# Seven block products in place of eight for the U and Z groups 0 to 3 of a hybrid decoder layer's input projection, made for two token tiles at a time

## The chip, the cores and the metric

The kernel runs on one core of one Trainium2 chip. The metric is the device time of one execution in microseconds (us), the median of several runs. The profile, taken by the hardware profiler, is of one such execution. The engines are called as in the profile: PE is TensorE (matrix products; PEld are its weight loads), DVE is VectorE, ACT is ScalarE, POOL is GpSimd, and SP is SyncE, whose queue issues nearly all DMA transfers here. L12 is line 12 of the kernel's file. Lines of the changed kernel are named as such, since its file is longer.

## What is computed

One decoder layer on 2048 tokens of width 1024, in f32. The part that the change touches is the input projection and the gMLP group; the rest is named because its work runs in the same stretches.

```
h = rms_norm(x, pre_norm_g)                       # (2048, 1024)
proj = h @ w_in                                   # 1024 -> 3072 columns
a_u, a_v, sq, sk, sv, mq, z = split(proj, [512, 512, 256, 128, 128, 256, 1024])
y_a = chunked_spatial_gating(gelu(a_u), gelu(a_v), ...)      # (2048, 512)
y_b = sliding_window_attention(sq, sk, sv, ...)              # (2048, 256)
y_c = memory_cross_attention(mq, mem_k, mem_v)               # (2048, 256)
y = concat(y_a, y_b, y_c) * silu(z)               # (2048, 1024)
x = x + rms_norm(y @ w_out, post_norm_g)

def chunked_spatial_gating(u, v, ...):            # chunks of 128 tokens, 4 groups of 128 channels
    vhat = layer norm of v over each group, with gain and bias
    sv = einsum('gts,bnsgc->bntgc', tril(w_s), vhat) + b_s
    return u * sv
```

So for the channel groups g = 0 to 3 of 128 channels each, the output part is y = gelu(U_g) * sv_g * silu(Z_g), where U_g and Z_g are products of h with 128 columns of `w_in`. These eight products (four U, four Z) for every token are what the change computes in another way. The other four Z groups (4 to 7) belong to the two attentions.

## The kernel before

**Tiles and stages.** The 2048 tokens are worked in four tiles of 512 (`TS`, `NT`). In phase 1 each tile t goes through the same list of products: V (96 matmuls of 128x512, L752), then the groups sv, k, q0, q1, mq0, mq1, z4, z5 (tile 0 has four small projections of the memory tokens here, L427), then U_g, a small product sg (four 128x128 matmuls, the spatial gating) and Z_g for g = 0 and 1, z6, z7, and the same for g = 2 and 3. A group (`group`, L321) is one bank of 128 channels by 512 tokens, made by 24 matmuls: eight chunks of the 1024 input channels, and for each three passes, because every f32 operand is split into a rounded part ("hi") and the rest ("lo") and hi·hi, hi·lo and lo·hi are summed. `split` makes the two parts: ACT casts hi (L91), DVE or POOL subtracts for lo (L92). Between every six matmuls of a group there is a slot (`slot`, L855): a table (`A_SLOTS`) puts pieces of the attention units of this tile there, four window units and eight memory units, whose softmax is done by DVE and ACT between two pieces.

**The normalised input.** h of a tile is kept, split, in one of two buffers `hTs`. For the next tile it is made in eight chunks of 128 channels (`make_h`, L306: a product on DVE with the row of 1/rms values, called `bcs`, then a split). The 1/rms values are computed by token, stored to DRAM (`rstd_d`, L257) and loaded back, broadcast to all partitions, as `bcs` (L261). `NEXT_STATS`, `LOADS` and `MAKES` are tables of slots for these steps.

**The weights.** Each group's weights come as one unit of 128x1024. In tile 0 (V of tile 1) a unit is loaded raw (`wraw`), split into a ring of four buffers of 1 MB (`whl`) and stored split to DRAM (`split_d`, L181); in later tiles it is loaded split (L146). When a unit is begun, `weight_unit` (L166) asks for the one three units on.

**The elementwise end of a group.** U_g goes through a gelu (`gelu2`) and Z_g through a silu (`silu2`), both shared by ACT and DVE; DVE multiplies gate, U and Z (L896, L899), and the result is stored to DRAM (`yd`).

**Phase 2**, the output projection (L1123), reads `yd` and already works two tiles at a time with seven products of blocks in place of eight, 672 matmuls in all. Its weight operands, differences of blocks of `w_out`, are made in tiles 1 and 2 (`weight_operands`, L617), and the sums of y for its first pair in tile 3 (`first_sums`).

**What sets the order.** The order on PE and on the SP queue is the order in which the program is written. In phase 1 DVE, ACT and POOL are ordered by a scheduler ahead of the run; in phase 2 all are ordered as written. Each engine works its own list strictly in that order, and an instruction that waits holds up those behind it.

## Time and profile before

| what | value |
|---|---|
| median of three runs | 763.64 us (763.6, 763.64, 764.14) |
| span of the profiled execution | 762.2 us |
| PE busy | 753.2 us, 99% of the span, 3700 matmuls |
| DVE busy | 562.8 us, 74%, 1056 instructions |
| ACT busy | 396.9 us, 52% |
| POOL busy | 110.7 us, 15%, 122 instructions |
| tile 0 / 1 / 2 / 3 / phase 2 / tail | to 167.7 / 144.9 / 145.0 / 144.8 / 152.4 / 7.4 us |
| DMA | 194 MB, mean 254 GB/s |

The profiled execution's own time is its span, 762.2 us, and the 1.4 us to the median lie around the span. The page gives the busy time of each engine and the chain of work that ended last, followed back from the last instruction; the table of waits says which engine stood still for what; the windows give busy time for chosen stretches; a group row of the page or of the lines view gives how often one instruction was run, its busy time and its mean duration. Matmuls are pipelined, so that the mean duration in such a row is not the time from one matmul to the next.

### The profile page before, as it was taken

The numbers are of one execution on the slowest core, as the hardware profiler recorded it, in microseconds if no ns is written. First come the engines' busy times: TensorE is split into PE (matmuls) and PEld (weight loads), VectorE is DVE, ScalarE is ACT, GpSimd is POOL, SyncE is SP. The second block draws the span as 40 slices with busy tenths as digits, with TensorE's granted clock in tenths as the row PEclk, the third lists the DMA queues.
The fourth block names the chain that finished last, engine by engine and source line by source line (L and its number), as shares of the span: only waits on it lengthen the run. The fifth ranks groups of instructions, "written<-read, shape, count | busy, mean of one in ns | idle before, by whom it ended". The sixth has DMA issues, their size and how long they took to land.

```text
span 762.2 us, 10453 instructions
## 1 busy us (share of the span) xinstructions
PE 753.2 (99%) x3700; PEld 634.1 (83%) x3700; DVE 562.8 (74%) x1056; ACT 396.9 (52%) x865; POOL 110.7 (15%) x122
## 2 busy tenths in 40 slices
PE   9999999999999999999999999999999999999996
PEld 7878988888888888888888888888888888888884
DVE  6396889996658878754888788748976325885787
ACT  7687775654735654455465544644443233443341
POOL 0556221000203200011032000201300000020002
PEclk9999999999999999999999999999999999999999
DMA  9847387987477897927678968664574699937734
GB/s 331 306 159 278 131 288 244 346 306 279 145 263 275 296 322 287 314 79 276 229 269 301 345 233 343 200 244 164 156 246 149 223 397 398 362 104 283 277 137 193
DMA packets 54068, 193.95 MB, mean 254 GB/s; under 512 B 5468, under 2 KB 6017, under 8 KB 44801
## 3 DMA queue, kind: packets, MB, share of 16 engines
q1 hardware_dynamic: 53488, 192.70, 71.0%
q8 instruction: 29, 0.48, 0.3%
q10 hardware_dynamic: 528, 0.59, 0.2%
q14 instruction: 23, 0.18, 0.1%
HBM read 140.84 MB, written 52.44 MB: 254 GB/s over the span
## 4 chain that ended last, share of the span: by engine, by line
PE 99%; DVE 0%; issue 0%; DVEq 0%; POOL 0%; ACT 0%; ACTq 0%; POOLq 0%
PE g_z L321 23%; PE v L752 12%; PE g_u L321 12%; PE g_q L321 6%; PE g_mq L321 6%; PE Y_S L1123 6%; PE Y L1123 6%; PE X_S L1123 6%; PE g_k L321 3%; PE X L1123 3%; PE g_sv L321 3%; PE l_b L497 2%; PE l_c L550 2%; PE o_b L532 2%; PE o_c L579 2%; PE sg L891 2%
## 5 line engine op out<-in xcount | busy, mean ns | idle before, releaser
L321 PE MATMUL g_z<-hT,whl 128*128 128x512 f32 x768 | 190.8, 396 | 0.0
L321 PEld LDWEIGHTS g_z<-hT,whl 128*128 128x128 f32 x768 | 139.6, 188 | 26.5
L321 PE MATMUL g_u<-hT,whl 128*128 128x512 f32 x384 | 96.5, 395 | 0.0
L752 PE MATMUL v<-whl,hT 128*128 128x512 f32 x384 | 89.4, 393 | 0.0
L752 PEld LDWEIGHTS v<-whl,hT 128*128 128x128 f32 x384 | 72.8, 190 | 15.8 <-ACT whl L91 0.6
L321 PEld LDWEIGHTS g_u<-hT,whl 128*128 128x128 f32 x384 | 69.9, 188 | 13.4
L91 ACT CAST whl<-wraw 128x1024 fp32r<-128x1024 f32 (+1 forms) x43 | 44.2, 1027 | 33.1 <-DMA wraw<-in_wst 15.3
L191 POOL TENSOR_TENSOR rsr_v<-rsa_v,mhalf 128x4 f32<-128x4 f32 x16 | 16.7, 1056 | 224.8 <-DVE mv L777 130.8
L321 PE MATMUL g_q<-hT,whl 128*128 128x512 f32 x192 | 45.9, 394 | 0.0
L92 DVE TENSOR_TENSOR whl<-wraw,whl 128x1024 fp32r<-128x1024 f32 (+1 forms) x30 | 35.5, 1183 | 12.7 <-ACT whl L91 12.5
L321 PE MATMUL g_mq<-hT,whl 128*128 128x512 f32 x192 | 44.7, 389 | 0.0
L1123 PE MATMUL Y_S<-hT,yop_S 128*128 128x512 f32 x192 | 44.2, 389 | 0.0
L1123 PE MATMUL Y<-hT,yop 128*128 128x512 f32 x192 | 43.8, 389 | 0.0
L522 POOL TENSOR_SCALAR_AFFINE_SELECT pT_b<-pT_b 128x512 fp32r<-128x512 f32 x30 | 21.3, 710 | 147.4 <-ACT pT_b L91 147.4
L1123 PEld LDWEIGHTS Y<-hT,yop 128*128 128x128 f32 x192 | 36.0, 188 | 7.5
L1123 PEld LDWEIGHTS Y_S<-hT,yop_S 128*128 128x128 f32 x192 | 36.0, 188 | 7.5
L321 PEld LDWEIGHTS g_q<-hT,whl 128*128 128x128 f32 x192 | 35.8, 188 | 7.8 <-ACT KK L91 0.2
L560 ACT ACTIVATE L_c<-l_c,nm_c 128x256 f32<-128x256 f32 x48 | 22.4, 471 | 37.8 <-DVE nm_c L555 37.8
L321 PEld LDWEIGHTS g_mq<-hT,whl 128*128 128x128 f32 x192 | 35.8, 188 | 7.3
L1028 POOL TENSOR_TENSOR r<-a,mhalf 128x1 f32<-128x1 f32 x16 | 13.5, 845 | 191.7 <-DVE a L1026 185.7
L92 POOL TENSOR_TENSOR whl<-wraw,whl 128x1024 fp32r<-128x1024 f32 x13 | 31.6, 2439 | 31.7 <-ACT whl L91 31.3
L992 DVE TENSOR_TENSOR yop<-y,yop 128x1024 fp32r<-128x1024 f32 x12 | 14.6, 1219 | 24.0 <-ACT yop L983 24.0
(211 smaller groups left out, 1427.1 us busy)
## 6 DMA issues: line engine op xcount, KB each, us to landing
whl<-split_d SPq DMA_DIRECT2D x50, 1024.0 KB, 6.3
wraw<-in_wst SPq DMA_DIRECT2D x41, 512.0 KB, 5.7
split_d<-whl SPq DMA_DIRECT2D x18, 1024.0 KB, 7.1
hT<-wo_B SPq DMA_DIRECT2D x10, 1024.0 KB, 8.7
wo_T<-hT SPq DMA_DIRECT2D x8, 1024.0 KB, 9.0
y<-yd SPq DMA_DIRECT2D x7, 1024.0 KB, 10.9
xj<-in_xT SPq DMA_DIRECT2D x12, 512.0 KB, 8.5
xs<-in_x SPq DMA_DIRECT2D x24, 256.0 KB, 5.6
```

Of the source, the lines that this page charges most:

```text
L91: a = nc.scalar.copy(hi, src)
L92: b = (lo_engine or nc.vector).tensor_tensor(lo, src, f32(hi), ALU.subtract)
L191: nc.gpsimd.tensor_tensor(r, a, mhalf[:, :c], ALU.pow)
L321: nc.tensor.matmul(ps, w[:, wi, k * P : (k + 1) * P], hT[:, hi, k, :], start=(n == 0), stop=(n == 3 * KC - 1))
L497: nc.tensor.matmul(lg[:, e, :], S[kv][:, e, c * P : (c + 1) * P], KK[:, kv, s, c * P : c * P + 256], start=(s == 0), stop=(s == 1))
L522: nc.gpsimd.affine_select(prev[:, s], f32(own[:, s]), [[0, 4], [-1, P]], ALU.is_gt, 0.0, base=0, channel_multiplier=1)
L532: nc.tensor.matmul(o[:, kv, :], SV[:, c + w, kv].rearrange("p a b -> p (a b)"), pT, start=(n == 0), stop=(n == len(terms) - 1))
L550: nc.tensor.matmul(lg[:, e, :], S[:, h % 2, q0 : q0 + P], MK[:, h, s, :], start=(s == 0), stop=(s == 1))
L560: last = nc.scalar.activation(p[:, e, :], lg[:, e, :], AF.Exp, bias=nm[:, e : e + 1], scale=scale, accum_out=den[:, e : e + 1])
L579: nc.tensor.matmul(o, MV[:, j, h].rearrange("p a b -> p (a b)"), pT[:, s, j].rearrange("p a b -> p (a b)"), start=(n == 0), stop=(n == 3))
L752: nc.tensor.matmul(vps[i], hT[:, hi, 2 * j + kk, i * P : (i + 1) * P], w[:, wi, kk * 512 : (kk + 1) * 512], start=(j == 0 and (hi, wi, kk) ...
L1123: nc.tensor.matmul(banks[m], a(s, k)[:, m * P : (m + 1) * P], w(v, k), start=first and n == 0, stop=n == 11, skip_group_check=not first)
```

## The change

U_g and Z_g for g = 0 to 3 are no longer made tile by tile. After tile 1, and again after tile 3, one function (`set_a`) makes them for both tiles of the pair. The weights are seen as a 2x2 matrix of blocks (U or Z, first or second half of the 1024 input channels), and h likewise (first or second half of the channels, first or second tile). The product of the two is made by seven block products, in the form of Strassen's scheme that Winograd gave, each with 4 groups x 12 matmuls of 128x512: 336 matmuls for a pair, where 2 tiles x 8 groups x 24 = 384 stood. Four of the seven are accumulated one after the other in the same four banks, with copies taken between; the last three are interleaved by group and end in the gelu, silu and products.

What else this brings with it:

- Sums and differences of the weight blocks, four 128x512 operations on POOL per group (`weight_sums`), made once, stored to DRAM (`tu_d`, `tz_d`) and read back in both sets. The 14 weight units of a set are loaded raw and split each time.
- Sums and differences of blocks of h (`h_sums`), 32 operations of 128x512 per pair, shared by POOL and DVE; three of the four sums are stored to DRAM and read back (12 transfers of 256 KB each way for a pair), and all four are split again.
- h of both tiles of a pair has to be held, so the two buffers become four half-buffers and a spare, and h of tile 0, overwritten by the memory's, is made a second time in tile 1.
- The normalised V (`vhat`) is stored to DRAM, by ACT's queue, and read back for the sg products, which now stand inside the set.
- The weight ring has three buffers, and in tile 0 the spare as a fourth. `weight_unit` refills the buffer of the unit that has just been used.
- For t > 0 the product of the softmax with 1/denominator goes from DVE to POOL (`normalise`). Gate·U·Z goes from DVE to POOL (`times`). The output projection's weight differences, now all in tile 2, and the sums of y in phase 2 go from DVE to POOL as well.
- The order of the seven products in phase 2 is another, and two of its first y operands are made in tile 3.
- The tables of slots are new. The first tile has eight groups fewer after its memory projections, so that h of tile 1 is made at its slots 32 to 42, where V of tile 1 begins at slot 36; before, the row of 1/rms values was loaded at slot 52, h made from slot 60, and V began at slot 68.

```diff
-NEXT_STATS = (16, 4)
-LOADS = ((46, 46, 48, 48, 53, 55, 65, 65), (34, 34, 36, 36, 43, 45, 57, 57))
-MAKES = ((60, 62, 64, 66, -28, -28, -24, -24), (50, 52, 55, 57, -28, -28, -24, -24))
+N_SLOTS = (36, 84, 28, 84)
+NEXT_STATS = (-8, 10, -23)
+MAKES = ((32, 33, 35, 36, 38, 39, 41, 42), (66, 68, 70, 72, 76, 79, 85, 88), (20, 22, 24, 26, 29, 31, 33, 35))
...
+LAST_SEQ = (("T1", 0), ("B21", 0), ("T1", 1), ("B22", 0), ("B21", 1), ("T1", 2),
+            ("B22", 1), ("B21", 2), ("T1", 3), ("B22", 2), ("B21", 3), ("B22", 3))
+FIRST_OPS = ("B11", "T2", "T3", "T4")
+SEQ_A = tuple((op, g) for op in FIRST_OPS for g in range(4)) + LAST_SEQ
...
-        while halved[0] < min(i + 4, len(order)):
+        if i - 1 in in_use:
+            place = in_use.pop(i - 1)
+            if place is not spare_ring or order[i][1] == 0:
+                free.append(place)
+        while halved[0] < len(order) and free:
...
+    def normalise(t, last, p, den, shape):
+        r = nc.vector.reciprocal(den, den)
+        scaled = (nc.gpsimd if t else nc.vector).tensor_tensor(p, p, den[:, :, None].broadcast_to(shape), ALU.mult)
+        queue_aside(last, r if t else scaled)
...
+    def weight_sums(g):
...
+        def difference(into, i, a, ia, b, ib):
+            c = [slice(512 * x, 512 * x + 512) for x in (i, ia, ib)]
+            nc.gpsimd.tensor_tensor(r[into][:, c[0]], r[a][:, c[1]], r[b][:, c[2]], ALU.subtract)
...
+        for n, x in enumerate((("u", 0, "z", 0, "u", 0), ("z", 0, "z", 1, "z", 0),
+                               ("z", 1, "z", 1, "u", 0), ("u", 1, "u", 1, "z", 1))):
+            yield s + 6 + 2 * n, lambda x=x: difference(*x)
...
+    def set_a(p):
...
+        def product(n, banks, first, then):
+
+            op, g = SEQ_A[n]
+            if n % 2 == 0:
+                held["w"] = weight_unit("A", n // 2, t1)
+            w = pair_of(held["w"])[:, n % 2]
+            i = 0
+            for k in range(4):
+                for wi, hi in ((0, 0), (0, 1), (1, 0)):
+                    nc.tensor.matmul(banks[g], w[:, wi, k * P : k * P + P], at_slot(places[op], hi, k),
+                                     start=first and i == 0, stop=i == 11, skip_group_check=not first)
+                    i += 1
+                if k == 1:
+                    slot()
+            then(g, banks[g])
+            slot()
...
+        def times(x, y):
+            nc.gpsimd.tensor_tensor(x, x, y, ALU.mult)
...
+        def end_z1(g, bank):
+            times(U[g], silu2(added(u3[g], bank), f"z{t1}_{g}", "G", 2))
+            store_later(yd[t1, g], U[g], 6)
+
+        def end_u0(g, bank):
+            x = gelu2(added(c1[g], bank), f"u{t0}_{g}", c1[g])
+            times(c1[g], gate[t0, g])
+
+        def end_z0(g, bank):
+            times(c1[g], silu2(added(u2[:, g], bank), f"z{t0}_{g}", "G", 2))
+            store_later(yd[t0, g], c1[g], 6)
...
+    def h_sums(p):
...
+            yield s, lambda k=k: whole("22", d, k, *bcs, nc.gpsimd)
+            yield s + 1, lambda k=k: whole("21", c, k, *e, nc.vector)
+            yield s + 2, lambda k=k: combine("22", "22", "21", k, ALU.add, "S1", nc.gpsimd)
+            yield s + 3, lambda k=k, third=third: whole("11", a, k, *third, nc.vector)
+            yield s + 4, lambda k=k: combine("21", "11", "21", k, ALU.subtract, "S3", nc.vector)
+            yield s + 5, lambda k=k: combine("11", "22", "11", k, ALU.subtract, None, nc.gpsimd)
+            yield s + 5, lambda k=k, fourth=fourth: whole("12", b, k, *fourth, nc.vector)
+            yield s + 6, lambda k=k: combine("12", "12", "11", k, ALU.subtract, "S4", nc.gpsimd)
...
-        def gate_a(g):
...
-            nc.vector.tensor_tensor(af, af, U, ALU.mult)
-            slot()
-            Z = silu2(slotted(U_Z + g, f"z{t}_{g}"), f"z{t}_{g}", "G", 2)
-            nc.vector.tensor_tensor(af, af, Z, ALU.mult)
```

Three places show how the instructions' order changes.

On PE, where the first two of the U and Z groups ended in tile 0, the program before had (`g_z_1` and `g_z_6` are groups, `l_c`, `tp_c`, `o_c` pieces of attention):

```order
L321 MATMUL g_z_1_1315<-hT_91,whl_11_1058 128x512 x12
L532 MATMUL o_b_3_1353<-pT_b_3_1259,SV 128x256 x8
L568 MATMUL tp_c_0_0_1368<-ident,L_c_0_0_1198 128x128 x4
L321 MATMUL g_z_1_1315<-hT_91,whl_11_1058 128x512 x6
L550 MATMUL l_c_1_1_1389<-MK,S_mq_0_668 128x256 x4
L321 MATMUL g_z_6_1407<-hT_91,whl_16_1142 128x512 x12
```

In the changed program the same kind of place, the beginning of the set after tile 1, reads (`X_0` are the banks of the four accumulated products, `hs_80`, `s4a` and `s4b` hold blocks of h or their sums):

```order
L822 MATMUL X_0_2356<-hs_80,ring_85 128x512 x12
L822 MATMUL X_0_2357<-hs_80,ring_85 128x512 x6
L619 MATMUL l_c_1_0_2486<-MK,S_mq_0_1951 128x256 x4
L822 MATMUL X_0_2357<-hs_80,ring_85 128x512 x6
L601 MATMUL o_b_3_2506<-pT_b_3_2422,SV 128x256 x8
L636 MATMUL tp_c_0_0_2521<-ident,L_c_0_0_2375 128x128 x4
L822 MATMUL X_0_2354<-s4a,ring_86 128x512 x6
L822 MATMUL X_0_2354<-s4b,ring_86 128x512 x6
```

Each bank now takes 12 matmuls of one weight block and is then left for the next group, and one unit of the ring serves two banks.

On DVE at the change from tile 0 to tile 1, the making of h for tile 1 stood before among the last U and Z groups of tile 0 (L306 is the product with `bcs`, and the lines into `hT_92` the lo part of the split):

```order
L306 SCALAR_TENSOR_TENSOR xj_0_1436<-xj_0_1436,colt,bcs_1560 128x512
L92 TENSOR_TENSOR hT_92<-xj_0_1436,hT_92 128x512
L330 TENSOR_TENSOR sc_u_3_1743<-g_u_3_1696,bcs_495 128x512
L893 SCALAR_TENSOR_TENSOR a_3_1756<-sg_3_1751,g_v,addend 128x512
L92 TENSOR_TENSOR hT_92<-xj_0_1436,hT_92 128x512
```

Now it stands among the last pieces of z6 and z7 (L371 is the product with the new `bcs_1108`, `hs_82` the buffer of h for tile 1, and L395 reads the finished group z7):

```order
L371 SCALAR_TENSOR_TENSOR xk_0_987<-xk_0_987,colt,bcs_1108 128x512
L545 RECIPROCAL den_b_3_1118<-den_b_3_1118 128x4
L606 TENSOR_TENSOR OB_773<-o_b_1_1186,oh_b_1_1195 64x2x128
L546 TENSOR_TENSOR Lc_b_3_1116<-Lc_b_3_1116,den_b_3_1118 128x4x128
L606 TENSOR_TENSOR OB_773<-o_b_1_1186,oh_b_1_1195 64x2x128
L109 TENSOR_TENSOR pT_b_2_1204<-tp_b_2_1199,pT_b_2_1204 128x512
L371 SCALAR_TENSOR_TENSOR xk_1_1030<-xk_1_1030,colt,bcs_1108 128x512
L624 TENSOR_REDUCE nm_c_0_0_1235<-l_c_0_0_1229 128x2
L109 TENSOR_TENSOR hs_82<-xk_0_987,hs_82 128x512
L395 TENSOR_TENSOR sc_z_7_1249<-g_z_7_1176,bcs_506 128x512
L626 TENSOR_TENSOR nm_c_0_0_1235<-nm_c_0_0_1235,rsr_x_271 128x2
L109 TENSOR_TENSOR hs_82<-xk_1_1030,hs_82 128x512
```

The lo part of the second chunk of h, which the first bank of V of tile 1 reads with its fourth matmul, has moved behind an instruction that reads the last product ahead of V. The sum of squares from which the new `bcs` comes (L252, the last row here) stands 21 rows ahead of the first of these:

```order
L574 SCALAR_TENSOR_TENSOR L_b_2_1_1007<-l_b_2_1_1002,rstd_q,bias 128x512
L575 TENSOR_TENSOR Lc_b_2_990<-L_b_2_0_999 128x2x128
L109 TENSOR_TENSOR s4a<-wraw_33_811,s4a 128x1024
L575 TENSOR_TENSOR Lc_b_2_990<-L_b_2_1_1007 128x2x128
L562 COPY Lc_b_3_1116<-sink_bc 128x4
L315 TENSOR_TENSOR ss_956<-ss_1_147 128x4
L576 TENSOR_REDUCE nm_b_2_991<-Lc_b_2_990 128x4
L252 TENSOR_SCALAR rsa_x_958<-ss_956 128x4
```

It stands behind the logits of the third window unit (`l_b_2_1`), which PE makes in the third of the four memory projections.

On POOL in tile 1 the program before had only the four selects of each window unit and a few small operations:

```order
L191 TENSOR_TENSOR rsr_v_3_2059<-rsa_v_3_2057,mhalf 128x4
L522 AFFINE_SELECT pT_b_0_2380<-pT_b_0_2380 128x512
L524 AFFINE_SELECT pT_b_0_2380<-pT_b_0_2380 128x512
L522 AFFINE_SELECT pT_b_0_2380<-pT_b_0_2380 128x512
L524 AFFINE_SELECT pT_b_0_2380<-pT_b_0_2380 128x512
L793 CAST SV<-SV 128x256
L522 AFFINE_SELECT pT_b_1_2479<-pT_b_1_2479 128x512
```

Now the sums of h (L898, L901) and the softmax's product (L546) stand between them:

```order
L546 TENSOR_TENSOR Lc_b_0_1959<-Lc_b_0_1959,den_b_0_1961 128x4x128
L901 TENSOR_TENSOR h_0_1_2085<-h_0_1_2030,h_0_1_2085 128x512
L901 TENSOR_TENSOR h_0_1_2122<-h_0_1_2122,h_0_1_2085 128x512
L901 TENSOR_TENSOR h_0_2_2169<-h_0_2_2169,h_0_2_2182 128x512
L898 TENSOR_TENSOR h_0_3_2302<-hs_83 128x512
L591 AFFINE_SELECT pT_b_0_2103<-pT_b_0_2103 128x512 x2
L593 AFFINE_SELECT pT_b_0_2103<-pT_b_0_2103 128x512 x2
L546 TENSOR_TENSOR Lc_b_1_2043<-Lc_b_1_2043,den_b_1_2045 128x4x128
L901 TENSOR_TENSOR h_0_2_2229<-h_0_2_2169,h_0_2_2229 128x512
```

Products and sums of two tensors have moved in ahead of the selects of the first window unit and between these and the next ones, and each select stands behind all that is ahead of it.

More of the change, by code (lines that the diff above doesn't have):

```diff
@@ new lines, in y_operand, with load, operand @@
+    def y_operand(src, slot, s, tag):
+        r = {}
+        def load():
+            r[0] = sp.tile([P, 4, TS], F32, tag=tag, name=f"yr_{slot}", bufs=1)
+            nc.sync.dma_start(r[0], src.rearrange("k p n -> p k n"))
+        def operand(k):
+            split(at_slot(slot, 0, k), at_slot(slot, 1, k), r[0][:, k], nc.gpsimd if k % 2 else nc.vector)
+        yield s, load
+        for k in range(4):
+            yield s + 5 + k, lambda k=k: operand(k)
+    jobs, stages, at = {}, {}, [0]
@@ new lines @@
+                if (p, name) in keep:
+                    o, cs = keep[p, name]
+                    nc.scalar.copy(o[m][:, cs], c)
+                do_work(step, True)
+                scaled = []
+                for os, ss, cs in ends.get((p, name), ()):
+                    o = os[m]
+                    if (p, name) == (0, "22"):
+                        squares(c, slice(0, 512), ss[m], 0)
+                        nc.vector.tensor_tensor(o[:, cs], c, gpost_bc[:, cs], ALU.mult)
+                    else:
+                        nc.vector.tensor_tensor(o[:, cs], c, o[:, cs], ALU.add)
+                        squares(o, cs, ss[m], int(cs is hi))
+                        scaled.append((o, cs))
```

778 lines of the change are left out of this document (459 added, 319 removed), and 3 rows, old and new, of the table LOADS.

## The prediction, made before the changed kernel was run

> **What bounds the kernel now.** I read the page first, for the busy shares and the chain that ended last, then the table of waits, then the chain's pieces.
>
> ```profile
> span 762.2 us, 10453 instructions
> PE 753.2 (99%) x3700; PEld 634.1 (83%) x3700; DVE 562.8 (74%) x1056; ACT 396.9 (52%) x865; POOL 110.7 (15%) x122
> PE 99%; DVE 0%; issue 0%; DVEq 0%; POOL 0%; ACT 0%; ACTq 0%; POOLq 0%
> ```
>
> ```profile
> PE warm L213 <- POOL ident masks.py:199: 1.5, 1, 1.5
> ```
>
> ```profile
> 79.17 4.32 PE gm L427 x36
> ...
> 167.73 21.76 PE v L752 x96
> ...
> 602.42 21.76 PE X_S L1123 x96
> ```
>
> PE never stands still after its start: the one wait in the table is for the constant of the warm-up. So the kernel is bound by PE, and the time is a number of matmuls times a pace. The pace is read from the chain: 96 matmuls of 128x512 in 21.76 us are 226.7 ns each, in phase 1 (V) and in phase 2 alike. The 256-column ones go at 4.32 / 36 = 0.12 us. The group rows would mislead here:
>
> ```profile
> L321 PE MATMUL g_z<-hT,whl 128*128 128x512 f32 x768 | 190.8, 396 | 0.0
> ```
>
> 396 ns is how long one is in the pipeline; 768 of them would be 304 us by it, while the row's own busy time is 190.8.
>
> How much room the others have is seen by stage (columns: stretch, its length, then busy time and count of PE, PEld, DVE, ACT, POOL, the granted clock, the DMA engines' share, GB/s):
>
> ```profile
> 95.00:167.70 72.70, 72.70 (x388) 62.04 (x387) 67.66 (x122) 46.89 (x110) 9.62 (x13) 1.00 0.83 290
> 167.70:312.60 144.90, 144.90 (x726) 122.43 (x725) 111.07 (x222) 77.18 (x182) 16.23 (x22) 1.00 0.77 270
> 602.40:754.80 152.40, 152.34 (x673) 125.80 (x671) 103.69 (x152) 59.41 (x111) 12.45 (x15) 1.00 0.73 274
> 754.80:762.20 7.40, 0.00 (x0) 0.00 (x0) 4.08 (x7) 0.72 (x2) 1.07 (x2) 0.76 0.55 212
> ```
>
> The granted clock is 1.00 throughout. DVE at 93% (67.66 of 72.70) still cost PE nothing. The profiled execution is 762.2, and the median 763.6 lies 1.4 above it; I add the same 1.4 after.
>
> **What is removed.** The listing of the changed program has 96 matmuls of 128x512 fewer (768 + 384 for Z and U become 384 + 2 x 336) and every other product as before. That is 96 x 226.7 ns = 21.76 us. If PE still never waits, the span is 762.2 - 21.8 = 740.4 and the time 741.9. The start and the tail of 7.4 us keep their work. What remains is what could make PE wait.
>
> **The change from tile 0 to tile 1.** This I expect to be late. The row of 1/rms values goes to DRAM and comes back. Before:
>
> ```profile
> 135.06 0.32 SPq L257 DMA_DIRECT2D rstd_d<-rsr_x  x1
> ...
> 142.50 0.32 SPq L261 DMA_DIRECT2D bcs<-rstd_d  x1
> ```
>
> The load waits for the store to land; each has its line in the view of its tile, the store first:
>
> ```profile
> DMA to landing us min/median/max: 6.1/7.3/10.3
> ```
>
> ```profile
> DMA to landing us min/median/max: 6.1/7.1/7.2
> ```
>
> So 14.4 us pass from the store to the landed row; before, 32.7 us lay between the store and V at 167.73. Now count from the start of z6. Between the end of l_b_2 and z6 stand 36 memory matmuls at 0.12 (4.3 us) and about 10 small ones of attention (1 us), so l_b_2 ends at -5.3. DVE then has the eight rows that end with the sum of squares (L252 of the changed kernel): a logits row, the lo part of a weight unit at 1.18, two halves at 0.42, a reduction at 0.69 and small ones, about 4.0, to -1.3. POOL's power takes 1.1:
>
> ```profile
> L191 POOL TENSOR_TENSOR rsr_x<-rsa_x,mhalf 128x4 f32<-128x4 f32 x4 | 4.5, 1124 | 23.3 <-DVE nm_c L557 14.5 <-DVE rsa_x L189 8.7
> L92 DVE TENSOR_TENSOR whl<-wraw,whl 128x1024 fp32r<-128x1024 f32 (+1 forms) x30 | 35.5, 1183 | 12.7 <-ACT whl L91 12.5
> L505 DVE TENSOR_REDUCE nm_b<-Lc_b 128x4 f32<-128x516 f32 x16 | 11.0, 685 | 0.2
> ```
>
> The store goes at -0.2 and the row is there at 14.2. Behind it DVE has twelve rows to the lo part of the second chunk: two products with `bcs`, three copies or sums, two lo parts, a softmax product and four small ones. Their spacing is that of this timeline, 0.66 after an operation on two SBUF tensors and 0.60 after one on PSUM:
>
> ```profile
> 159.75 0.73 DVE L306 SCALAR_TENSOR_TENSOR xj<-xj,colt,bcs 128x512 f32<-128x512 f32 x1
> 160.41 0.67 DVE L92 TENSOR_TENSOR hT<-xj,hT 128x512 fp32r<-128x512 f32 x1
> 161.01 0.67 DVE L330 TENSOR_TENSOR sc_u<-g_u,bcs 128x512 f32<-128x512 f32 x1
> 161.61 0.73 DVE L893 SCALAR_TENSOR_TENSOR a<-sg,g_v,addend 128x512 f32<-128x512 f32 x1
> ```
>
> That is 6.1 us, to 20.3. PE has 48 matmuls of z6 and z7 (10.9) and 2.9 of attention, is at V at 13.8 and needs this chunk with V's fourth matmul, at 14.5. It waits 5.8 us. With both transfers at their shortest (6.1) it is 3.6, at their longest 8.7. If DVE lags elsewhere in this stretch, PE's attention pieces are late too: the 35 to 42 us from z6 to the end of V carry 16 chunks of h (tile 1's eight and tile 0's again) at 2 x 0.63, 20 us of DVE where there were 10. Bounds 3 and 11; I take 5.8.
>
> **DVE and POOL.** POOL gets about 190 operations of two SBUF inputs, counted at 128x512, for 13 splits of 128x1024 before. Their price is half of the first row here, 1.2 us; the second is a select:
>
> ```profile
> L92 POOL TENSOR_TENSOR whl<-wraw,whl 128x1024 fp32r<-128x1024 f32 x13 | 31.6, 2439 | 31.7 <-ACT whl L91 31.3 <-POOL SV L793 0.5
> L522 POOL TENSOR_SCALAR_AFFINE_SELECT pT_b<-pT_b 128x512 fp32r<-128x512 f32 x30 | 21.3, 710 | 147.4 <-ACT pT_b L91 147.4
> ```
>
> It is 230 us of POOL in a span in which it was idle for 650. POOL's own time is no bound, but what it does to DVE may be. Two timelines at one place, POOL's and DVE's, and the row of DVE's operation there:
>
> ```profile
> 78.99 2.40 POOL L92 TENSOR_TENSOR whl<-wraw,whl 128x1024 fp32r<-128x1024 f32 x1 [2.99 <-ACT whl L91]
> ```
>
> ```profile
> 79.74 1.93 DVE L504 TENSOR_TENSOR Lc_b<-L_b 128x256 f32<-128x256 f32 x1
> ```
>
> ```profile
> L504 DVE TENSOR_TENSOR Lc_b<-L_b x30: 412/424/1926, 79.7 to 536.0; 128x256 f32<-128x256 f32 x30
> ```
>
> An operation of 424 ns took 1.93 us; it ended 0.28 us after POOL's, at 81.67. I read it as waiting until POOL had done. The Trainium skill says so outright (SBUF — State Buffer, "Who interferes with whom"): a DVE operation with two SBUF inputs and a GpSimd one share a pair of ports, and whoever starts first holds it for the whole instruction. The trace agrees (424 ns became 1926), and the rule speaks against this change.
>
> The fullest stretch is tile 1 from its sv product to the first block product: 67 us of PE. DVE's rows there, at the spacings above, come to 54 us, of which 26 are 52 operations on two SBUF tensors; POOL has 22 sums and products (26 us), 12 selects (8.5) and three powers (3), 38 us in all. Taken one after the other, the port is used 26 + 38 = 64 of 67 us. How much DVE is held up: an operation of its 52 finds POOL busy in 38/67 = 0.57 of cases and waits for half of a 1.2 us operation, 18 us in all, which makes 54 + 18 = 72 of 67. So DVE would end this stretch some 5 us behind; the set that follows has 41 us of DVE in its first 56, which gives that back before anything late, but PE's attention pieces in between may wait. I take 2, between 0 and 10. The last 12 block products (36 us) have 33 of DVE and 25 to 29 of POOL and then V of tile 2, where DVE has 21 in 51; tile 3's set is alike. I take 1 each, between 0 and 6. In phase 2 POOL gets sums of about 39 us beside 104 - 12 of DVE in 152, with two or three steps of 5.4 us to spare; I take nothing there, 3 if that cover is gone.
>
> **Weights and DMA.** Loaded units land in time so far (the tile of the split weights):
>
> ```profile
> DMA to landing us min/median/max: 4.7/6.5/9.7
> ```
>
> With three buffers a unit is asked for two units ahead, 2 x 24 x 0.2267 = 10.9 us, where it was three (16.3). 9.7 still fits. In tile 2 the listing has 27.6 MB in about 75 us, 370 GB/s. What the queue can do is shown where it is full:
>
> ```profile
> 420.00:440.00 20.00, 20.00 (x106) 16.92 (x105) 15.29 (x28) 10.38 (x27) 0.00 (x0) 1.00 1.00 340
> 620.00:640.00 20.00, 20.00 (x90) 16.57 (x89) 9.45 (x13) 6.17 (x9) 0.00 (x0) 1.00 1.03 403
> ```
>
> At 403 it is hidden; at 340 the 27.6 MB take 81 us, 6 too many, of which the buffers ahead hide some 2 MB. It lies between the two rows and nearer to neither: 0 taken, 0 to 6 as bounds. The Trainium skill gives a peak of about 436 GB/s (SBUF — State Buffer, "SBUF: two separate sides"); by it, too, nothing would be lost, and no row here reaches it.
>
> **Sum.** 741.9 + 5.8 + 2 + 2 x 1 = 751.7, said as 752. Its own range is 746 (3.6 at the change of tiles and nothing else) to 758 (8.7, 5 and 2).
>
> **Rivals.**
>
> 1. PE stays full, or all but: 742 to 745. For it: no wait before, with DVE at 93%. Against it: the two transfers alone are 12.2 us at their shortest, and with DVE's rows they end 3.6 us late. It needs the sum of squares earlier on DVE than its rows say.
>
> 2. POOL makes DVE the bound. Each DVE operation held up also holds the ones behind it, those on PSUM too. If in tile 1 the two engines took turns completely, 54 + 38 = 92 us would stand in 67, 25 late; the same in tile 3 before its set (52 + 36 in 59) 29. With one of the two in full, or both by half, it is 25 to 30 us: 742 + 25 = 767 to 772, slower than before. It decides from the point where the hold-ups pass 13 us in tile 1 (67 - 54), 0.25 us for each of the 52 operations; my 18 is beyond that point by 5, and only the slack in the next stretch keeps this from being the forecast. A middle of it is 761 to 767. For it: the row at 79.74. Against it: 28 of the 54 us have a PSUM input, and the pieces of one attention unit stand five and more slots apart, 8 us and more.
>
> 3. The ring of three buffers, or the queue in tile 2: where transfers go at 307 GB/s (the mean of the two windows' lower one and the 274 of phase 2), 27.6 MB take 90 us, 15 too many: 742 + 15 = 757, with the change of tiles 763. For it: fewer buffers, 211 MB for 194. Against: the landing times above.
>
> That the change doesn't remove what it says is excluded by the counts.
>
> **How the numbers follow.** Forecast 0.45, rival 1 0.25, rival 2 0.20 (slower 0.09, the same 0.05, faster 0.06), rival 3 0.10 (slower 0.02, same 0.01, faster 0.07). A measurement of this kernel tells 0.2%, 1.5 us, from no change (the three runs lie within 0.5). So faster is 0.45 + 0.25 + 0.06 + 0.07 = 0.83, the same 0.06, slower 0.11. The range, 742 to 763, leaves out about 0.02 below and the 0.14 of rival 2 and 3 above it.
>
> **What would show it.** The table of waits of the changed kernel should name V (L1067) at the change from tile 0 to tile 1, waiting for the lo part of h on DVE, 4 to 9 us, and the view of `bcs` a store about 14 us before its first use. DVE's two-SBUF rows (L575, the lo parts from SBUF) should have maxima of 1 us and more where POOL works, and their means rise, while those on PSUM stay. If the waits are short and the time is above 752, the matmuls' pace would have changed, which I hold to be 226.7 ns. If waits of PE for pieces of the softmax or for selects (L601, L636) add up to more than 10 us in tiles 1 and 3, rival 2 is the case. Waits on weights in the ring or in the sets would show rival 3.

## The result: 68 us slower

The changed kernel takes 832.28 us (median of four runs, 829.04 to 833.44), the kernel before 763.89 in the runs beside it. The ratio is 1.089, with a 95% interval of 1.0868 to 1.0911. Predicted were 752 us, with a range of 742 to 763: the sign was wrong.

The profiled execution's span is 827.0 us. The page's first lines, and its chain of work that ended last by engine:

```profile
span 827.0 us, 10835 instructions
PE 761.2 (92%) x3604; PEld 629.1 (76%) x3604; DVE 624.9 (76%) x1028; ACT 439.4 (53%) x941; POOL 381.6 (46%) x293
PE 49%; DVE 27%; DMA 13%; issue 3%; ACT 3%; POOL 3%; SPq 2%; DVEq 0%; ACTq 0%; POOLq 0%
```

The matmuls are the 96 fewer that were counted (3700 to 3604). But PE is no longer the whole chain: DVE has 27% of it. DVE has 28 instructions fewer than before and is busy 62 us more. The table of PE's waits, which had one line before (columns: who waited for whom, us in total, times, longest):

```profile
PE o_b L601 <- POOL pT_b L593: 9.0, 9, 2.1
PE X L1377 <- DVE ring L1234: 4.4, 1, 4.4
PE o_b L601 <- POOL pT_b L591: 4.1, 4, 2.0
PE v L1067 <- ACT hs L108: 3.8, 2, 2.3
PE tp_c L636 <- DVE L_c L546: 3.5, 1, 3.5
...
PE v L1067 <- DMA ring<-split_d: 2.4, 2, 1.7
...
PE g_z L386 <- DMA ring<-split_d: 1.8, 1, 1.8
PE g_q L386 <- DMA ring<-split_d: 1.7, 1, 1.7
```

No one wait is large. There are some forty of them, for pieces of attention (o_b, tp_c, o_c), for h (v), in the sets, for weights (DMA ring) and in phase 2 (X L1377). By stage, the windows of the changed kernel (columns as before: stretch, length, busy time and count of PE, PEld, DVE, ACT, POOL, granted clock, DMA share, GB/s) show where:

```profile
78.50:113.70 35.20, 31.14 (x195) 28.60 (x194) 28.89 (x51) 23.50 (x58) 12.18 (x11) 0.90 0.75 279
113.70:149.00 35.30, 31.73 (x158) 26.15 (x157) 32.99 (x60) 19.57 (x43) 12.30 (x13) 0.95 0.85 310
149.00:239.90 90.90, 76.33 (x343) 61.46 (x342) 79.16 (x147) 45.42 (x112) 51.03 (x40) 0.92 0.70 234
239.90:297.40 57.50, 57.50 (x294) 48.44 (x293) 41.12 (x67) 42.69 (x94) 16.22 (x18) 1.00 0.63 191
297.40:344.90 47.50, 42.49 (x210) 34.98 (x209) 42.57 (x49) 16.89 (x26) 30.96 (x18) 0.96 0.56 182
...
366.70:439.90 73.20, 66.17 (x305) 53.77 (x303) 52.09 (x111) 41.80 (x105) 34.10 (x33) 0.95 0.86 315
...
475.80:550.50 74.70, 70.02 (x346) 57.55 (x345) 66.70 (x130) 40.77 (x99) 42.35 (x35) 1.00 0.77 282
...
656.60:819.20 162.60, 154.37 (x673) 126.77 (x671) 108.66 (x134) 63.39 (x118) 61.73 (x36) 0.99 0.66 244
```

They are, in order: the memory projections, z6 and z7; V of tile 1; tile 1 from sv to the first block product; the set's four accumulated products; its last twelve products; tile 2 from sv to the next V; tile 3 from sv to the first block product; phase 2. Of these rows of phase 1 the fourth, 239.9 to 297.4, is the only one where PE is full, and POOL has little to do there (16 of 57 us). PE's work in a stretch is its matmuls at the pace that they have without waits. Tile 1's stretch took 91 us for 67 us of PE's work, the same stretch of tile 3 only 75 for 68. Phase 2, 152.4 before, took 162.6 for the same 672 matmuls.

Behind some of the waits the granted clock is 0.50, and that is a loss of its own: in the trace there are nine such stretches, of 3.4 or 6.8 us each, before the tail. The first row is a stretch of matmuls right behind two waits:

```profile
172.60:177.30 4.70, 4.70 (x13) 3.63 (x11) 4.70 (x11) 3.63 (x7) 1.37 (x1) 0.50 0.97 311
345.10:366.80 21.70, 21.70 (x97) 17.96 (x96) 11.86 (x18) 5.91 (x11) 10.31 (x8) 1.00 0.83 303
```

At a clock of 0.50 two matmuls start 427 ns apart; the second row is V of tile 2, at 1.00 and the old pace. Not every wait is followed by it: behind one of 3.5 us, which ended at 182.35, the matmuls of 128x512 were at the old pace of about 227 ns from the second on. The Trainium skill (TensorE: Matmul & The Clock Gate, Part 1) gives 426.7 ns from start to start for 512 columns while the array is cold, its word for the slow clock; the trace agrees. Adding up the distances between matmul starts over the trace, PE stood still some 70 us longer than before and lost some 16 us to the half clock. Together that is the 86.6 us between 827.0 and the 740.4 without waits.

What DVE lost is seen in its rows. One and the same form of instruction, first with one input in PSUM (`g_z`), then with both in SBUF (`u` is the sum kept there), and two more with both in SBUF:

```profile
L670 DVE SCALAR_TENSOR_TENSOR Z_z<-Z_z,g_z 128x512 f32<-128x512 f32 x12 | 8.1, 678 | 0.1
L670 DVE SCALAR_TENSOR_TENSOR Z_z<-Z_z,u 128x512 f32<-128x512 f32 x16 | 19.2, 1199 | 5.2 <-ACT Z_z L669 5.2
L109 DVE TENSOR_TENSOR hs<-xj,hs 128x512 fp32r<-128x512 f32 x16 | 14.6, 929 | 0.2
L1234 DVE TENSOR_TENSOR yop<-y,yop 128x1024 fp32r<-128x1024 f32 x10 | 18.8, 1883 | 24.3 <-ACT yop L1229 24.3
```

The first takes 678 ns, the second 1199; the lo part of h, 681 before, takes 929; the y operand, 1219 before, takes 1883. POOL pays too:

```profile
L901 POOL TENSOR_TENSOR h<-h,h 128x512 f32<-128x512 f32 x24 | 36.7, 1535 | 16.8 <-DVE h L901 7.3 <-issue 4.2 <-DVE h L898 3.1
```

That is 1535 on average where 1220 was reckoned. The shortest of the 24 took 1263, so a little of the difference is a price set too low, and most of it is not.

### The profile page after: what moved, and what is told of

Same layout as the page of the kernel before. It is cut to its first block, busy times and chain, and to the rows that moved or that the text cites. A ratio compares the mean times of both kernels' runs of the same rounds, so it can differ in the third digit from the quotient of the medians.

```text
span 827.0 us, 10835 instructions
## 1 busy us (share of the span) xinstructions
PE 761.2 (92%) x3604; PEld 629.1 (76%) x3604; DVE 624.9 (76%) x1028; ACT 439.4 (53%) x941; POOL 381.6 (46%) x293
## 4 chain that ended last, share of the span: by engine, by line
PE 49%; DVE 27%; DMA 13%; issue 3%; ACT 3%; POOL 3%; SPq 2%; DVEq 0%; ACTq 0%; POOLq 0%
PE X L822 10%; PE X L1377 8%; PE v L1067 7%; PE Y_S L1377 5%; PE g_mq L386 3%; PE g_q L386 2%; DVE hs L109 2%; DMA ring<-split_d 2%; PE g_z L386 2%; DVE h L898 2%; DMA gpost_bc<-in_gpost 2%; DMA bcs<-rstd_d 1%; DMA wo<-in_wst 1%; DVE xj L371 1%; DMA wraw_a<-in_wst 1%
## 5 line engine op out<-in xcount | busy, mean ns | idle before, releaser
L1067 PE MATMUL v<-ring,hs 128*128 128x512 f32 x336 | 85.6, 407 | 9.2 <-ACT hs L108 3.8
L386 PE MATMUL g_z<-hs,ring 128*128 128x512 f32 x360 | 90.3, 401 | 1.8 <-DMA ring<-split_d 1.8
L1067 PEld LDWEIGHTS v<-ring,hs 128*128 128x128 f32 x336 | 63.7, 195 | 25.0 <-ACT hs L108 4.5
L386 PEld LDWEIGHTS g_z<-hs,ring 128*128 128x128 f32 x360 | 67.4, 193 | 15.4 <-DMA ring<-split_d 2.2
L822 PE MATMUL X<-hs,ring 128*128 128x512 f32 x288 | 71.9, 398 | 0.0
L822 PEld LDWEIGHTS X<-hs,ring 128*128 128x128 f32 x288 | 52.9, 190 | 10.2
L546 POOL TENSOR_TENSOR L_c<-L_c,den_c 128x512 f32<-128x512 f32 x24 | 27.0, 1127 | 61.0 <-DVE den_c L545 58.4
L1270 POOL TENSOR_TENSOR r<-a,mhalf 128x1 f32<-128x1 f32 x16 | 13.2, 826 | 70.2 <-DVE a L1268 67.2
L386 PE MATMUL g_q<-hs,ring 128*128 128x512 f32 x168 | 43.7, 412 | 1.7 <-DMA ring<-split_d 1.7
L386 PE MATMUL g_mq<-hs,ring 128*128 128x512 f32 x192 | 44.7, 389 | 0.0
L901 POOL TENSOR_TENSOR h<-h,h 128x512 f32<-128x512 f32 x24 | 36.7, 1535 | 16.8 <-DVE h L901 7.3
L386 PEld LDWEIGHTS g_mq<-hs,ring 128*128 128x128 f32 x192 | 35.8, 188 | 7.3
L1234 DVE TENSOR_TENSOR yop<-y,yop 128x1024 fp32r<-128x1024 f32 x10 | 18.8, 1883 | 24.3 <-ACT yop L1229 24.3
L601 PE MATMUL o_b<-pT_b,SV 128*128 128x256 f32 x124 | 24.3, 326 | 13.3 <-POOL pT_b L593 9.0
L1377 PE MATMUL X<-hs,ring 128*128 128x512 f32 x120 | 31.6, 399 | 4.4 <-DVE ring L1234 4.4
L601 PEld LDWEIGHTS o_b<-pT_b,SV 128*128 128x128 f32 x124 | 20.1, 219 | 18.8 <-POOL pT_b L593 11.9
L1377 PE MATMUL X<-hs,yop 128*128 128x512 f32 x120 | 31.3, 396 | 2.8 <-DVE yop L1234 2.8
L1377 PE MATMUL Y_S<-hs,yop 128*128 128x512 f32 x144 | 33.1, 389 | 0.0
## 6 DMA issues: line engine op xcount, KB each, us to landing
hs<-wo_B SPq DMA_DIRECT2D x8, 1024.0 KB, 14.1
y<-yd SPq DMA_DIRECT2D x8, 1024.0 KB, 12.5
```

What stands on the lines that cost most here:

```text
L386: nc.tensor.matmul(ps, w[:, wi, k * P : (k + 1) * P], h(t, hi, k), start=(n == 0), stop=(n == 3 * KC - 1))
L546: scaled = (nc.gpsimd if t else nc.vector).tensor_tensor(p, p, den[:, :, None].broadcast_to(shape), ALU.mult)
L601: nc.tensor.matmul(o[:, kv, :], SV[:, c + w, kv].rearrange("p a b -> p (a b)"), pT, start=(n == 0), stop=(n == len(terms) - 1))
L822: nc.tensor.matmul(banks[g], w[:, wi, k * P : k * P + P], at_slot(places[op], hi, k), start=first and i == 0, stop=i == 11, skip_group_che ...
L901: engine.tensor_tensor(r[into, k], r[x, k], r[y, k], op)
L1067: nc.tensor.matmul(vps[i], h(t, hi, 2 * j + kk)[:, i * P : (i + 1) * P], w[:, wi, kk * 512 : (kk + 1) * 512], start=(j == 0 and (hi, wi, k ...
```

## The experiments

Three theories stood. A: POOL and DVE hold each other up at SBUF. B: data come late that make a round trip through DRAM, or weights in a ring of three buffers. C: plain overload or POOL's queue, selects behind long operations. Single runs are told with their time; those with an interval had four runs.

**POOL's new work cut short.** In the changed kernel, the in-place two-tensor operations of POOL in phase 1 get 4 to 16 columns of each 512; for example

```diff
-            nc.gpsimd.tensor_tensor(x, x, y, ALU.mult)
+            nc.gpsimd.tensor_tensor(x[:, 0:16], x[:, 0:16], y[:, 0:16], ALU.mult)
```

and the same for the softmax's division, the sums of h and of weight blocks, and the output weights' differences.

> The changed kernel with POOL's in-place operations on two tensors of phase 1 cut to 4 to 16 of each 512 columns. It leaves out most of the softmax's division in tiles 1 to 3, of the sums of h and of weight blocks and of gate times U times Z; every instruction, its place in the program, its dependencies and all DMA stay. Theory A (POOL and DVE hold each other up at SBUF): the 70 us of PE standing still and 16 us of slow pace after it fall to the parts that have nothing to do with POOL (the change from tile 0 to tile 1, the transfers, the beginning of phase 2), 20 to 30 us: 762 to 775 us. Theory B (data that make a round trip through DRAM, or weights in a ring of three buffers, come late): POOL's time changes little, 810 to 830 us.

Measured: 788.14 us, 44 less. The page:

```profile
PE 749.1 (95%) x3604; PEld 622.6 (79%) x3604; DVE 568.9 (72%) x1028; ACT 437.3 (56%) x941; POOL 241.1 (31%) x293
```

DVE has the same 1028 instructions and is busy 56 us less (624.9 to 568.9): those 56 us were not work. Tile 1's stretch falls from 90.9 to 74.6:

```profile
147.80:222.40 74.60, 70.52 (x342) 57.21 (x341) 62.80 (x143) 41.91 (x102) 23.78 (x40) 1.00 0.83 283
```

The result lies between the two expectations. Of the 86.6 us over the span without waits 41 come with POOL's work in phase 1 (the span went from 827.0 to 786.1); the other 46 do not. The run takes away POOL's own time as well as what it does to DVE, and does not tell the two apart.

**POOL's work alone, in the kernel before.** To separate the holding-up from everything else in the change, the kernel before got extra work on POOL that nothing depends on, at each slot of tiles 1 to 3:

```diff
-    ctx.enter_context(tc.manual_schedule(engines={mybir.EngineType.PE, mybir.EngineType.SP}))
+    ctx.enter_context(tc.manual_schedule(engines={mybir.EngineType.PE, mybir.EngineType.SP, mybir.EngineType.Pool}))
...
+            if t:
+                nc.gpsimd.tensor_tensor(dz.rearrange("p (a b) -> p a b", a=2), bias[:, 0:2, :], bias[:, 2:4, :], ALU.mult)
```

> The kernel before, with one more POOL product of two SBUF tensors of 128x512 (a constant, into a scratch tile that nobody reads) at each of the 180 slots of tiles 1 to 3, and POOL's order as written; nothing else is changed, no engine but POOL gets work. Theory A: DVE's operations on two SBUF tensors wait behind these 216 us of POOL (180 x 1.2) and PE begins to wait: 790 to 830 us. Theory B: 764 to 768 us. If only the selects are late, behind five of these at a time (6 us, of the 8 us between the pieces of an attention unit): 764 to 780 us.

> As the run of 180 extra products, with two POOL fills of the 128x512 scratch tile (write only, no input) in the place of each product. Theory A, if it is the reading of SBUF that counts: DVE's durations stay as before and the time is 764 to 770 us. If any work of POOL holds up DVE, or if the queue of POOL alone makes the selects late: 780 us and more, near the run with products.

> The kernel before with the extra POOL products of two tensors at every second slot of tiles 1 to 3, 90 in the place of 180. The run with fills gave 777 and that with 180 products 845. If every product costs its share, 777 + 34 = 811 us; if there is slack that has to be used up first, as theory A has it where DVE is busy 72 to 76%: 780 to 795 us.

> The kernel before with POOL's order as it is written in place of the scheduler's, and nothing added. In the runs with extra POOL work PE waited 10 to 12 us once in tile 0 for a weight's lo part on POOL, ahead of any extra product. If that comes from the order, this run has it too and takes 775 to 778 us, and POOL's fills cost nothing; if it comes from the extra work, 764 us.

| kernel before, POOL's order as written, and | us |
|---|---|
| nothing added | 777.03 |
| 360 fills (write only) of 128x512 | 777.35 |
| 90 products of two SBUF tensors | 807.07 |
| 180 products of two SBUF tensors | 844.59 |

POOL's order by itself costs 13 us (one wait in tile 0, for a weight's lo part), and stands in all four. Fills cost nothing beyond that (their run had 764 to 770 expected, without these 13), though they kept POOL busy for 190 us; products cost 30 us for 90 and 67.6 for 180. The rows of the fills and of the 180 products, and under each DVE's softmax product (two SBUF inputs) and lo part from PSUM in the same run. With fills:

```profile
L871 POOL MEMSET dz<- 128x512 f32 x180 | 95.0, 528 | 10.4
L566 DVE TENSOR_TENSOR L_c<-L_c,den_c 128x512 f32<-128x512 f32 x32 | 22.8, 714 | 1.0
L92 DVE TENSOR_TENSOR pT_c<-tp_c,pT_c 128x512 fp32r<-128x512 f32 x32 | 21.9, 685 | 0.2
```

With 180 products:

```profile
L870 POOL TENSOR_TENSOR dz<-bias 128x512 f32<-128x512 f32 x180 | 261.6, 1454 | 12.8
L566 DVE TENSOR_TENSOR L_c<-L_c,den_c 128x512 f32<-128x512 f32 x32 | 33.5, 1047 | 1.0
L92 DVE TENSOR_TENSOR pT_c<-tp_c,pT_c 128x512 fp32r<-128x512 f32 x32 | 21.8, 682 | 0.3
```

Of these two, only the row with two SBUF inputs stretches (714 to 1047 ns), the one with a PSUM input does not (685 and 682), and only POOL's reading does it. The other rows of the two runs agree: DVE's frequent forms with a PSUM input stay within 1%, forms with two SBUF inputs in tiles 1 to 3 take up to twice as long (the lo part of the output weights 715 and 1455 ns). A small copy with one SBUF input is an exception (296 and 590). That is theory A by itself, without any of the change. It speaks against POOL's queue alone making the selects late: the fills filled that queue as well, though for 190 us where the products took 262, and with 180 products PE waited 30 us for DVE and 8 for selects. The longest line:

```profile
PE o_c L582 <- DVE pT_c L92: 21.4, 7, 4.9
```

The Trainium skill (SBUF — State Buffer, "Who interferes with whom") says that a DVE instruction with two SBUF inputs contends with a GpSimd instruction that reads SBUF, not with one that only writes it; the runs agree (777.35 us with the fills, 777.03 without). The 180 products took the kernel past the 790 to 830 that theory A expected. For 90, of the two cases of the expectation the first (811, each product its share) was nearly met, and the slack of theory A (780 to 795) was not there: the first 90 cost 0.33 us each on average, the next 90 0.42.

**The same work on DVE.** All of it, or the softmax's division alone:

```diff
-            nc.gpsimd.tensor_tensor(x, x, y, ALU.mult)
+            nc.vector.tensor_tensor(x, x, y, ALU.mult)
...
-        scaled = (nc.gpsimd if t else nc.vector).tensor_tensor(p, p, den[:, :, None].broadcast_to(shape), ALU.mult)
+        scaled = nc.vector.tensor_tensor(p, p, den[:, :, None].broadcast_to(shape), ALU.mult)
```

> The changed kernel with all that it gave to POOL done by DVE: the softmax's division, the sums of h and of weight blocks, gate times U times Z, the lo parts in the sets, the output weights' differences and the sums of y. Theory A: DVE gets about 190 x 0.66 = 125 us more and loses its hold-ups (60 us), 690 us busy of 760 to 790, unevenly spread; PE waits for DVE in tile 1 and in the sets, but less than now: 765 to 800 us. Theory B: 825 us or more.

> The changed kernel with the softmax's division back on DVE in all tiles: 36 operations, 41 us of POOL's time go and 24 us of DVE's come. Theory A: POOL's operations hold up more of DVE than they take over, and 41 of its 230 us are some 18% of the 41 us that the run with short POOL operations gained: 7 us less, 822 to 828 us. If DVE is as full as POOL (theory of plain overload), no change or slower: 830 to 838 us.

All on DVE: 809.17 us, 23 less than the changed kernel and 45 more than the one before, between the two expectations. Three of DVE's rows that had stretched in the changed kernel (1199, 929 and 1883 ns) are then:

```profile
L670 DVE SCALAR_TENSOR_TENSOR Z_z<-Z_z,u 128x512 f32<-128x512 f32 x16 | 11.0, 688 | 0.8 <-ACT Z_z L669 0.7
L109 DVE TENSOR_TENSOR hs<-xj,hs 128x512 fp32r<-128x512 f32 x16 | 10.8, 684 | 0.0
L1234 DVE TENSOR_TENSOR yop<-y,yop 128x1024 fp32r<-128x1024 f32 x10 | 12.2, 1221 | 22.7 <-DMA s4b<-wo_B 13.7 <-ACT yop L1229 9.0
```

The same instructions on the same data, without POOL's new work beside them, have the durations of the kernel before again. The division alone: 833.04 (831.26 to 839.02), no change that can be told from 832.28; of its two expectations the second (830 to 838) came. Tile 1's stretch with all on DVE:

```profile
151.10:232.40 81.30, 72.38 (x344) 59.36 (x343) 77.31 (x169) 44.03 (x105) 14.03 (x15) 0.96 0.74 260
```

With all on DVE that engine is busy 77.3 of 81.3 us: it has no hold-ups from POOL's sums, and is full with work. So the elementwise work fits neither engine in this stretch: beside POOL it holds DVE up, and on DVE alone it is more than PE's 67 us. With the division alone on DVE the stretch takes 94.3 us, and DVE is busy for 81 of them: that move bought nothing.

**The change from tile 0 to tile 1.**

```diff
-NEXT_STATS = (-8, 10, -23)
+NEXT_STATS = (-16, 10, -23)
```

> The changed kernel with the sums of squares and the row of 1/rms for tile 1 eight slots earlier (-16 for -8). By the prediction's step on the change of tiles this takes away the wait for the row, 4 to 6 us of PE's waits at the beginning of V and 1 to 2 us of slow pace after them: 824 to 828 us. If V waits for DVE for other reasons there: 830 us or more.

Measured: 845.82 (839.05 to 848.7), 13 us slower. PE's waits there, first in the changed kernel, then with this edit, from 40 to 130 us:

```profile
PE gm L492 <- ACT s4a L108: 3.0, 1, 3.0
PE v L1067 <- ACT hs L108: 2.3, 1, 2.3
PE v L1067 <- DVE hs L109: 1.3, 2, 0.8
```

```profile
PE g_mq L386 <- ACT ring L108: 7.4, 1, 7.4
PE gm L492 <- DVE s4a L109: 2.3, 1, 2.3
PE v L1067 <- DVE hs L109: 1.2, 2, 0.8
```

V's wait falls from 3.6 us (2.3 for ACT's hi part, 1.3 for DVE's lo part) to 1.5 (the 1.2 shown, and 0.3 for ACT), as expected of an earlier row. But the squares that it needs now stand among ACT's casts of the weights for mq, and PE waits 7.4 us for those. In this stretch PE's waits add up to 13.3 us, where 7.7 stood. V's wait did come from the late row, as the step on the change of tiles has it, and the edit moved the wait to a place where it is longer.

**Phase 2, and the edits together.**

```diff
+    at(0, lambda: nc.sync.dma_start(gpost_bc, gpost.broadcast_to([P, D])))
     at(0, load_y, "12", 0)
...
-    at(1, lambda: nc.sync.dma_start(gpost_bc, gpost.broadcast_to([P, D])))
```

> The changed kernel with the broadcast load of the output gains issued as the first transfer of phase 2 and not behind four of 1 MB. If the beginning of phase 2 loses its time because DVE stands before this load: the 9 us of PE's waits there go, with 1 us of slow pace, 821 to 825 us. If the y operands would be late without it too (held up by POOL's sums): 828 to 832 us.

> The three edits together (load of the gains first, 1/rms eight slots earlier, the softmax's division on DVE), and the sums of y in phase 2 on DVE again. If the causes are separate their gains add: 6 to 9, 4 to 7 and 5 to 9, and for the sums of y 1 to 4: 803 to 816 us. If one wait only takes another's place, less than half of that: 818 us or more.

The load first: 833.24 (831.98 to 835.98), no gain, as in the second of its expectations. In the changed kernel the chain runs through this load for 13 us; with the load ahead, the chain of the same place reads

```profile
675.92 15.09 DMA y<-yd
...
700.54 2.70 DVE ring L1234
```

A y load of 15 us and three DVE operations of 2.3 to 2.8 us took its place. The four edits together: 836.95 (834.41 to 839.27), nothing gained in all, though phase 2 itself, with the sums of y on DVE, came down from 162.6 to 156.0:

```profile
669.80:825.80 156.00, 153.16 (x672) 125.64 (x671) 106.00 (x149) 62.83 (x117) 15.72 (x18) 1.00 0.68 254
```

What it gained was lost again elsewhere, in tile 0 among others, where PE waits 6.8 us for weight casts among the earlier squares.

**The transfers, and what is left.** Half of the columns of each output-weight operand are stored and loaded:

```diff
-            store_later(wo_d[op][j], f32(w), 4)
+            store_later(wo_d[op][j][:, :, 0:512], f32(w[:, :, 0:512]), 4)
```

> The changed kernel with only the first half of the columns of each output-weight operand stored and loaded (the second halves of those operands are what lay in the place before; 7 MB of stores less in tile 2, 14 MB of transfers less in all). Its tile 2 (from sv to the next V) takes 73 us where its PE work is some 63. If transfers make it wait there: PE's waits for ring loads (5.9 us in the changed kernel) fall under 1.5, tile 2 comes to 66 to 69 and the time to 820 to 826 us. If the loads are late for the ring of three buffers alone: the waits stay, 828 to 834 us.

Measured: 824.24, inside the first of the two ranges, but not by the mechanism that it stood for. The waits for ring loads became

```profile
PE g_q L389 <- DMA ring<-split_d: 2.7, 1, 2.7
PE g_z L389 <- DMA ring<-split_d: 1.8, 1, 1.8
```

4.5 us where 5.9 stood. V of tile 3 lost its wait, q and z of tile 2 kept theirs, and tile 2 as a whole was no shorter (76.7 us, where I had expected 66 to 69). What was gained lies elsewhere, most of it in V of tile 3 (30.6 us for 35.9) and phase 2. The transfers are at most a part of it; with half of the stores gone the loads still come late, which speaks for the ring of three buffers, but that was not tried by itself.

The last run puts three things together: POOL's operations short (the in-place sums of y too), the transfers halved, the gains' load first.

> The changed kernel with POOL's in-place operations cut short (as in the first run, and the in-place sums of y too), the output-weight operands stored and loaded by halves, and the load of the gains first. It leaves out the parts named there. If POOL with DVE, the transfers of tile 2 and the beginning of phase 2 are the three causes beside the change of tiles, what is left is the 742 without waits and 10 to 20 us: 755 to 765 us. If there is a cause not yet named: 772 us or more.

Measured: 773.6 us. Phase 2 is back at 152.1:

```profile
611.50:763.60 152.10, 152.10 (x673) 125.93 (x671) 90.75 (x130) 62.47 (x116) 27.56 (x33) 1.00 0.59 209
111.80:148.00 36.20, 33.01 (x157) 27.17 (x157) 32.08 (x61) 19.38 (x43) 9.16 (x15) 0.91 0.83 301
```

Of the 86.6 us 55.6 are gone (827.0 to 771.4). The 31 that are left are spread: V of tile 1 is still 36 us long for some 29 of PE's work (second row), tile 1 from sv on still 74 for 67, and the memory projections, tile 2 and the two sets lose some 5 to 7 us each. The expectation had at most 20 and took 772 us or more as the mark of a cause not yet named. That mark was reached, so the causes of this rest stay open.

Even with this work left out the kernel stays 10 us behind the one before, so none of these edits points to a version that beats it.

## Why the prediction was wrong

- **What bounds the kernel, and the 21.8 us.** Right: 96 matmuls went, and where PE is not held up it still has its pace (V of tile 2, 97 in 21.7 us).
- **The change from tile 0 to tile 1.** The chain was right, its price too small. The chain in the changed kernel, and then the landings of its stores and loads in the view of `rstd_d`:

```profile
100.31 11.77 DMA bcs<-rstd_d
...
116.30 1.02 DVE hs L109
...
118.00 0.61 DVE hs L109
...
118.65 3.66 PE v L1067 x9
```

```profile
DMA to landing us min/median/max: 1.4/2.6/11.8
```

  z6 began at 99.56. The row landed 12.5 us after that (reckoned: 14.2), the second lo part was ready at 19.0 (20.3), V came up at 14.1 (13.8). That the row came so near to its time is in part luck: the store went 3.1 us ahead of z6 (reckoned: 0.2) and landed in 1.4 us (7.3), and the load, issued 2.5 us after that, took 11.8 (7.1). PE waited 3.6 us there in all, where 5.8 stood, and 2.3 of these were for ACT's hi part, which the step did not count; the sign that was named, 4 to 9 us for the lo part on DVE, did not show. PE then made its first nine matmuls in 3.66 us. What was missed is that half clock behind the wait, and a wait of 4 us two groups earlier, for the memory projections' weights. From these projections to the end of V 70.5 us passed for some 57 of PE's work: 13 lost, where the sum has 5.8. (The longest case of this step is 8.9 by its own numbers, not 8.7: 10.3 + 7.2 in place of 14.4.)

- **DVE and POOL: the step that failed.** The forecast had the mechanism, the price of an operation and even the hold-ups in tile 1 (18 us on top of 54), and then let them be given back: "the set that follows has 41 us of DVE in its first 56, which gives that back before anything late", hence 2 us, with 10 as the bound for attention pieces that come late. Measured, DVE was busy 79 us in that stretch (so 25 of hold-ups), POOL 51 in place of 38, and PE took 91 us for 67. Two things were wrong in the step. A backlog of DVE is not given back later: PE's list is fixed and has a piece of attention at nearly every slot, so PE stands at the first piece that is late, and from there on PE is as late as DVE. PE lost its 24 us inside the stretch; the set behind it, 57.5 us for 57 of work, could give none of them back. And POOL is held up as well as DVE (1535 ns, 1263 at the shortest), which makes its hold on DVE longer in turn; how much of the 25 this is was not measured. The second rival was the true case. Its sign, waits of more than 10 us for the softmax and the selects (L601, L636) in tiles 1 and 3, came to 17.7 us, and its full price for tile 1, 25 us, was right to 1 us. I gave it 0.20, and its total, 767 to 772, was still 60 us short. For tile 3 it had 29 where 7 were lost, and why tile 3 did so much better was not followed up. What it lacked came in other places: the last products of the sets (47.5 and 42.7 us for some 40 of PE's work; the prediction had 36), tile 2, phase 2 and the half clock.
- **Average slack.** "DVE at 93% still cost PE nothing" was read as slack. The run with 90 products shows little or none: with DVE at 72% on average, the added POOL products cost 0.33 us each. A schedule in which PE never waits shows only that every piece was in time, not by how much.
- **Phase 2.** "I take nothing there, 3 if that cover is gone": 10 us. Sums reckoned at 2.4 us on POOL took 2.4 to 3.1, y operands of 1.2 took 1.9, and loads queued behind one another at its beginning. With the sums of y on DVE and the load moved it is 156.0; with the in-place sums cut short, the load moved and the weights' transfers halved it is 152.1, and what the sums alone are worth was not tried.
- **Weights and DMA.** "0 taken, 0 to 6": 5.9 us of waits, and 11 us in tile 2 with all that it shares. The landing times were those of the kernel before. In the changed kernel the longest load took 13.2 us, not 9.7:

```profile
DMA to landing us min/median/max: 4.8/6.7/13.2
```

  That is more than the 10.9 us that the prediction gave a ring of three buffers, and less than the 16.3 of the ring before.
- **The pace.** "226.7 ns" was held to be fixed. Behind some of the waits it was 427 ns for some us, 16 us in all, which on average adds a quarter to a microsecond of waiting here (16 for 70).

## What to carry to other kernels

Fewer matmuls by sums of blocks pay in elementwise work: here 21.8 us of PE were bought with some 190 operations of 128x512 on POOL and nearly as many instructions on DVE as before (1028 for 1056), and neither engine had the room, wherever they were put. Before giving POOL work that reads SBUF, count DVE's operations with two SBUF inputs in the same stretch; a POOL product beside a busy DVE cost 0.33 to 0.42 us of the kernel's time here, a fill nothing. And a chain in which the bounding engine never waits is no proof of slack: put a dummy load on the engine that is to get more work and read what each operation of it costs.

## What the runs showed that was not expected

The cost of POOL's products was nearly in proportion to their number (30.0 us for 90, 67.6 for 180); whether there is a threshold below 90 was not tried. Four edits, each at a place where the trace named the wait, gained nothing together (836.95 for 832.28). And an edit that shortened V's wait made the kernel 13 us slower: in the profiled executions PE's waits at that place rose by 5.6 us, with a new one of 7.4 for weight casts that ACT now had among the squares, and the rest of the 13 was not followed up.
